# Two-layer hybrid decoder trunk on one core: modulation weights in a load ring of their own, weight tiles in a ring of five, stores put off

## The chip, the cores and the metric

The kernel runs on 1 core of one Trainium2 chip. The metric is the device time of one execution in microseconds (us); several runs are taken and their median is quoted. A profiled execution is a single one; its span is the time from its first to its last instruction.

## What is computed

Two layers over 256 tokens of width 2048, batch 1, all in float32. Each layer normalises its input, scales and shifts it by vectors that come from a conditioning vector `c` ("adaLN"), projects it, runs two mixers side by side on the result, merges them and adds the residual:

```python
def hybrid_layer(x, c_act, pos, norm_w, ada_w, ada_b, w_in, ret_gn_w, sinks, w_ret_o, w_swa_o, w_out):
    shift, scale, gate = jnp.split(c_act @ ada_w + ada_b, 3, axis=-1)
    u = rms_norm(x, norm_w) * (1.0 + scale[:, None, :]) + shift[:, None, :]
    proj = u @ w_in
    rq, rk, rv, rg, sq, sk, sv, sg, mg_ret, mg_swa = jnp.split(proj, offsets, axis=-1)
    ...
    ret_y = r @ w_ret_o          # r: chunkwise retention, group norm, SiLU gate
    ...
    swa_y = (a * jax.nn.silu(sg)) @ w_swa_o   # a: sliding-window attention with sinks
    merged = jax.nn.sigmoid(mg_ret) * ret_y + jax.nn.sigmoid(mg_swa) * swa_y
    return x + gate[:, None, :] * (merged @ w_out)
```

`c_act` is `silu(c)`, and the trunk ends with one more RMS norm. `ada_w` is 2048 x 6144 per layer, `w_in` 2048 x 15360, and the three output projections are 2048 x 2048 each.

## The kernel before, in words

**Weight steps.** The products with the weights are cut into chunks of 512 output columns, and a chunk into steps of two 128-row blocks of the weight (`steps`; in the sliced chunks some have one block). A step loads one tile of 128 x 1024 float32 (512 KB) from DRAM, and `prep` (L291) splits it into an upper half `w_hi` (ACT, L118) and a lower half `w_lo` = tile - upper half (DVE, L115). `gemm` (L307) then issues three products per pair of halves: 12 matmuls of 512 columns where tokens are the output's rows (token-major) and 24 of 256 where features are (feature-major: `qk`, `sq`, `sk`, `sg`). `prep` runs `LOOKAHEAD` = 3 steps ahead of the matmuls, and `w_hi` and `w_lo` have four buffers each.

**Order of chunks in a layer.** First the retention's twelve chunks (`qk`, `rg`, `rv` four times), in slices over the input features (four slices in layer 0, two in layer 1), so that the first products can start before all modulation vectors are there. Then `mr` (4 chunks), `ro` (4), `sk`, `sv`, `sq` and `sg` (4 each, in turn), `ms` (4), `so` (4), `wo` (4). The last chunk of `wo` is done half by half (`gemm_halves`, L343), so that the norm of the next layer can begin.

**Modulation.** `c_act @ ada_w` is done on the DVE: a unit is a 128 x 1024 tile of the transposed `ada_w`, multiplied by `c_act` and summed along its row (the reduce, L245). There are 192 units: 64 for layer 0's scale and shift, 32 for its gate, 64 for layer 1's scale and shift, 32 for its gate. `ada_block` (L214) issues a unit's load and its reduce together. `run_background` (L140), called after each step, issues them at a pace per step (`PACE`, `ada_pace`), beside the retention heads and the attention heads.

**Rings.** Pool tiles of one name share a ring of buffers, and a load waits until the buffer's last reader is done. Weight tiles and modulation tiles have the same name and pool,

```python
raw = state.get("ada_pool", wpool).tile([P, TK * NC], F32, name="w_raw")
SP.dma_start(out=raw, in_=src[i, :, h * 1024:(h + 1) * 1024])
```

with four buffers; only the 64 units of layer 0's scale and shift use a pool of eight (`adaraw`, which closes before the last slice).

**Queues.** Every DMA is issued by SP, in one list. The program's text is not the engines' order: the framework's scheduler lists each engine's instructions, and puts one that could run in an earlier gap of that engine, by its own estimates; on the chip each engine goes through its list strictly in order, waiting at each entry.

**Stores and fetches beside this.** `merge_first` (L648) stores the gated retention product `y1d[c]`; `merge_second` (L654) fetches it again in the output stage; the residual of layer 0 is stored in `hres` (L859) and fetched in layer 1.

Of the kernel before, what the change touches and what calls it, by code (L numbers as in the profile page):

```python
# [10 lines left out]
F32 = mybir.dt.float32  # L11
# [6 lines left out]
P = 128  # L18
# [14 lines left out]
PACE = (0.1, 0.6, 0.15, 0.4)  # L33

# [38 lines left out]
def trunk(ctx: ExitStack, tc: tile.TileContext, x, c2, earlyc, latec, win, wro, wso, wout, sinks, fnw, decayT,  # L73
# [8 lines left out]
    wpool, small = pool("wpool", 4), pool("small", 2)  # L82
    dpool = pool("dpool", space=DRAM)
# [46 lines left out]
    # ---------------------------------------------------------------- background work  # L130
# [60 lines left out]
    # ---------------------------------------------------------------- adaLN vectors  # L191
# [20 lines left out]
    gates = [dpool.tile([D], F32, name=f"gates{l}") for l in range(L)]  # L212

    def ada_block(key, l, src):  # L214
        nf = src.shape[0]
        part = small.tile([P, 32, 2], F32, name="ada_part")
        k0, k1 = (0, KT) if key[0] == "gate" else slice_bounds(l)[key[2]]

        def finish(f0, f1):
            p0, p1 = part[:, f0:f1, 0], part[:, f0:f1, 1]  # L220
            if key[0] == "gate":
                tt(p0, p0, p1, ALU.add)
                tt(p0, p0, adab_t[:, l, 32 + f0:32 + f1], ALU.add)
                ps = bank()
                PE.transpose(ps[0:KT, 0:P], p0, ident)
                row = small.tile([KT, P], F32, name="gate_row", bufs=1)
                ACT.activation(row, ps[0:KT, 0:P], AF.Copy)
                release(ps)
                SP.dma_start(out=gates[l].rearrange("(k p) -> k p", p=P), in_=row)
                return  # L230
            ks = slice(k0 + f0 // 2, k0 + f1 // 2)
            b = adab_t[:, l, 0:32].rearrange("p (a k) -> p k a", a=2)[:, ks, :]
            p0, p1 = (p.rearrange("p (k a) -> p k a", a=2) for p in (p0, p1))
            tt(p0, p0, b, ALU.add)
            tt(p0, p0, p1, ALU.add)
            DVE.scalar_tensor_tensor(out=scale[:, l, ks], in0=p0[:, :, 1], scalar=1.0, in1=norm_t[:, l, ks],
                                     op0=ALU.add, op1=ALU.mult)
            DVE.tensor_copy(out=shift[:, l, ks], in_=p0[:, :, 0])

        for f in range(0, nf, 2):  # L240
            for h in range(2):
                for i in (f, f + 1):
                    raw = state.get("ada_pool", wpool).tile([P, TK * NC], F32, name="w_raw")
                    SP.dma_start(out=raw, in_=src[i, :, h * 1024:(h + 1) * 1024])
                    DVE.tensor_tensor_reduce(out=raw, in0=raw, in1=c_row[:, h * 1024:(h + 1) * 1024], scale=1.0, scalar=0.0,  # L245
                                             op0=ALU.mult, op1=ALU.add, accum_out=part[:, i, h:h + 1])
                    yield 1.25
            if key == ("mod", 0, 0):
                finish(f, f + 2)
        if key != ("mod", 0, 0):  # L250
            finish(0, nf)
        done.add(key)
# [21 lines left out]
    # ---------------------------------------------------------------- products with the weights  # L274
# [15 lines left out]

    def prep(upto):  # L291
        while progress["prep"] < min(upto, len(steps)):
            i = progress["prep"]
            n, k, nk = steps[i]
            raw = wpool.tile([P, TK * NC], F32, name="w_raw")[:, 0:nk * NC]
# [11 lines left out]
    def gemm(act, ps=None):  # L307
# [6 lines left out]
        while progress["step"] < len(steps) and steps[progress["step"]][0] == n:  # L314
# [24 lines left out]
            run_background(STEP_BUDGET * nk / TK)  # L339
        flush()  # L340
        return ps

    def gemm_halves(act, finish):  # L343
# [3 lines left out]
        for t in range(2):  # L347
            ps = bank()
            for x in range(count):
# [3 lines left out]
                for j in range(TK):  # L353
                    kk = steps[i][1] + j
                    ah, al = (a[:, kk % 4, t * P:(t + 1) * P] for a in act[kk // 4])
                    for m, (a, w) in enumerate(((ah, hi), (al, hi), (ah, lo))):
                        mm(ps, a, w[:, j * NC:(j + 1) * NC],
                           x == 0 and j == 0 and m == 0, x == count - 1 and j == TK - 1 and m == 2)
                if t == 0:
# [7 lines left out]
    # ---------------------------------------------------------------- norm and modulation  # L367
# [32 lines left out]
    # ---------------------------------------------------------------- retention  # L400
# [101 lines left out]
    # ---------------------------------------------------------------- sliding-window attention  # L502
# [139 lines left out]
    # ---------------------------------------------------------------- gates and merges  # L642
# [5 lines left out]
    def merge_first(c, ps):  # L648
# [3 lines left out]
        SP.dma_start(out=y1d[c], in_=tokens(y))  # L652

    def merge_second(pl, c, ps, m_parts):  # L654
        yield from until(lambda: c == 0 or ("merged", c - 1) in keep)
        y1 = pl.tile([P, 1024], F32, name="stage", bufs=2)
        SP.dma_start(out=tokens(y1), in_=y1d[c])
        y = keep.pop(("ms", c))
        tt(y, ps, y, ALU.mult)
        tt(y, y, y1, ALU.add)  # L660
# [11 lines left out]
    # ---------------------------------------------------------------- schedule  # L672
# [4 lines left out]
    def ada_enqueue(key):  # L677
        ada_queue.append(ada_block(key, key[1], blocks[key]))
# [19 lines left out]
    with tc.tile_pool(name="start", bufs=1) as sp, tc.tile_pool(name="adaraw", bufs=8) as state["ada_pool"]:  # L698
        xt = [sp.tile([P, 2, NC], F32, name=f"x{c}") for c in range(4)]
        sums = sum_tiles()  # L700
        SP.dma_start(out=early, in_=earlyc)
        for _ in range(4):
            ada_turn()
        for c in range(4):
            SP.dma_start(out=xt[c], in_=xpart(c))
# [59 lines left out]
    for l in range(L):  # L765
# [65 lines left out]
        with tc.tile_pool(name=f"out{l}", bufs=1) as pl:  # L831
            m_parts = act_tiles(pl, "m")
            pace[0] = PACE[3]
# [11 lines left out]
            for c in range(4):  # L845
# [7 lines left out]
                def residual(t, ps, c=c, gr=gr, res=res):  # L853
# [4 lines left out]
                    if not last:  # L858
# [101 lines left out]
```

## Time and profile before

| what | value |
|---|---|
| runs | 2109.76, 2109.99, 2112.79 us; median 2109.99 us |
| span of the profiled execution | 2108.1 us |
| busy: PE, DVE, ACT, POOL | 2027.6, 1464.3, 1072.4, 19.1 us |
| moved by DMA | 480.78 MB, 228 GB/s in the mean |
| DMA issues of 512 KB weight tiles / modulation tiles | 660 / 192 |

The profiled execution's own time is the first to the last record; the runs are timed without a profile, and their median is 1.9 us longer than that span. PE is TensorE's matmul, DVE VectorE, ACT ScalarE, POOL GpSimd, SP SyncE. Matmuls are pipelined: a 512-column matmul is listed with some 0.39 us, and the next one starts 0.23 us after it.

### The profile page before, as it was taken

How to read it: one execution, taken by the hardware profiler on the slowest of the kernel's cores; microseconds unless marked ns; L12 is line 12 of the kernel's file. 1: busy time of each engine (PE TensorE's matmuls, PEld its weight loads, DVE VectorE, ACT ScalarE, POOL GpSimd, SP SyncE). 2: the span in 40 equal slices, each digit the busy share in tenths (PEclk: the TensorE clock that was granted, in tenths of full speed). 3: DMA queues.
4: the chain of work that ended last, by engine and by line, in shares of the span. 5: the costliest groups of instructions: out<-in, count | busy, mean ns of one | idle time of the engine just before them, and what ended most of it. 6: DMA issues, size and time to landing. Idle time of an engine off the chain costs nothing.

```text
span 2108.1 us, 30062 instructions
## 1 busy us (share of the span) xinstructions
PE 2027.6 (96%) x11482; PEld 1762.2 (84%) x11482; DVE 1464.3 (69%) x2115; ACT 1072.4 (51%) x1493; POOL 19.1 (1%) x28
## 2 busy tenths in 40 slices
PE   5999999999999999999998999999989999999998
PEld 3888888877899998877777898888778999988886
DVE  5899997666777777677656668864666677764555
ACT  4643556433465667534453545553334676674443
POOL 0000000000000000000000000000000000000000
PEclk7999999999999999999999999999999999999999
DMA  8989656678765666778868855556887554557664
GB/s 312 348 313 374 200 181 201 194 263 288 269 205 183 197 193 196 230 258 271 292 215 274 286 189 178 175 188 216 274 279 250 172 159 151 160 184 239 206 208 151
DMA packets 136595, 480.78 MB, mean 228 GB/s; under 512 B 15202, under 2 KB 15362, under 8 KB 136324
## 3 DMA queue, kind: packets, MB, share of 16 engines
q1 hardware_dynamic: 136452, 478.87, 68.5%
q8 instruction: 90, 1.47, 0.3%
q14 instruction: 53, 0.43, 0.1%
HBM read 470.41 MB, written 8.40 MB: 227 GB/s over the span
## 4 chain that ended last, share of the span: by engine, by line
PE 72%; DMA 15%; DVE 6%; issue 4%; ACT 2%; POOL 0%; SPq 0%; DVEq 0%; POOLq 0%; ACTq 0%
PE ps_mm L107 66%; DMA w_raw<-in_ada 10%; PE ps L107 4%; DVE w_lo L115 3%; DMA w_raw<-in_win 3%; ACT w_hi L118 2%; DMA w_raw<-in_wout 1%; DVE w_raw L245 1%; DMA w_raw<-in_wro 1%; PE ps L613 1%; PE ps L388 1%; DMA x<-in_x 0%; DVE sig L115 0%; ACT ps L370 0%; DVE sks L115 0%
## 5 line engine op out<-in xcount | busy, mean ns | idle before, releaser
L118 ACT ACTIVATE w_hi<-w_raw 128x1024 fp32r<-128x1024 f32 (+1 forms) x676 | 703.4, 1043 | 832.0 <-PE ps_mm L107 439.1
L115 DVE TENSOR_TENSOR w_lo<-w_raw,w_hi 128x1024 fp32r<-128x1024 f32 (+1 forms) x676 | 810.7, 1204 | 367.8 <-ACT w_hi L118 363.8
L107 PE MATMUL ps_mm<-uh,w_lo 128*128 128x256 f32 x1664 | 472.2, 284 | 8.5 <-DVE w_lo L115 8.3
L107 PE MATMUL ps_mm<-uh,w_hi 128*128 128x256 f32 x1664 | 472.7, 284 | 0.3 <-ACT w_hi L118 0.2
L107 PE MATMUL ps_mm<-ul,w_hi 128*128 128x256 f32 x1664 | 470.7, 283 | 0.0
L107 PE MATMUL ps_mm<-w_lo,uh 128*128 128x512 f32 x1088 | 429.7, 395 | 10.6 <-DVE w_lo L115 10.3
L107 PE MATMUL ps_mm<-w_hi,uh 128*128 128x512 f32 x1088 | 430.2, 395 | 2.4 <-ACT w_hi L118 2.4
L107 PE MATMUL ps_mm<-w_hi,ul 128*128 128x512 f32 x1088 | 427.4, 393 | 0.0
L245 DVE CUSTOM_DVE_ANT_0 w_raw<-w_raw,c_row 128x1024 f32<-128x1024 f32 x192 | 234.4, 1223 | 170.6 <-DMA w_raw<-in_ada 161.8
L107 PEld LDWEIGHTS ps_mm<-uh,w_lo 128*128 128x128 f32 x1664 | 319.0, 192 | 10.9 <-DVE w_lo L115 10.9
L107 PEld LDWEIGHTS ps_mm<-uh,w_hi 128*128 128x128 f32 x1664 | 319.0, 192 | 2.1 <-ACT w_hi L118 0.7
L107 PEld LDWEIGHTS ps_mm<-ul,w_hi 128*128 128x128 f32 x1664 | 319.0, 192 | 1.4
L107 PEld LDWEIGHTS ps_mm<-w_lo,uh 128*128 128x128 f32 x1088 | 206.0, 189 | 62.3 <-DVE w_lo L115 19.2
L107 PEld LDWEIGHTS ps_mm<-w_hi,uh 128*128 128x128 f32 x1088 | 206.5, 190 | 44.5 <-ACT w_hi L118 4.1
L107 PEld LDWEIGHTS ps_mm<-w_hi,ul 128*128 128x128 f32 x1088 | 206.5, 190 | 41.0
L107 PE MATMUL ps_mm<-w_lo,rah 128*128 128x512 f32 x512 | 202.8, 396 | 15.3 <-DVE w_lo L115 15.0
L107 PE MATMUL ps_mm<-w_hi,rah 128*128 128x512 f32 x512 | 201.9, 394 | 1.1 <-ACT w_hi L118 1.1
L107 PE MATMUL ps_mm<-w_hi,ral 128*128 128x512 f32 x512 | 200.3, 391 | 0.0
L107 PEld LDWEIGHTS ps_mm<-w_lo,rah 128*128 128x128 f32 x512 | 96.5, 188 | 43.9 <-DVE w_lo L115 23.7
L107 PEld LDWEIGHTS ps_mm<-w_hi,rah 128*128 128x128 f32 x512 | 96.7, 189 | 20.9 <-ACT w_hi L118 1.9
L107 PEld LDWEIGHTS ps_mm<-w_hi,ral 128*128 128x128 f32 x512 | 96.7, 189 | 20.1
L107 PE MATMUL ps_mm<-w_lo,mh 128*128 128x512 f32 x192 | 75.9, 395 | 0.0
(150 smaller groups left out, 1662.7 us busy)
## 6 DMA issues: line engine op xcount, KB each, us to landing
w_raw<-in_win SPq DMA_DIRECT2D x468, 512.0 KB, 4.2
w_raw<-in_ada SPq DMA_DIRECT2D x192, 512.0 KB, 5.5
w_raw<-in_wro SPq DMA_DIRECT2D x64, 512.0 KB, 4.9
w_raw<-in_wso SPq DMA_DIRECT2D x64, 512.0 KB, 3.6
w_raw<-in_wout SPq DMA_DIRECT2D x64, 512.0 KB, 4.7
w_raw<-in_win SPq DMA_DIRECT2D x24, 256.0 KB, 3.9
y1d<-sig SPq DMA_DIRECT2D x8, 512.0 KB, 5.4
stage<-y1d SPq DMA_DIRECT2D x8, 512.0 KB, 5.2
```

The costliest lines, as they stand in the source:

```text
L107: PE.matmul(o, lhsT=lhsT, rhs=rhs, start=start, stop=stop, skip_group_check=True)
L115: DVE.tensor_tensor(out=o, in0=a, in1=b, op=op)
L118: ACT.activation(hi, src, AF.Copy)
L245: DVE.tensor_tensor_reduce(out=raw, in0=raw, in1=c_row[:, h * 1024:(h + 1) * 1024], scale=1.0, scalar=0.0, op0=ALU.mult, op1=ALU.add, accu ...
L388: PE.transpose(ps[:, j * S + t * P:j * S + (t + 1) * P], h[:, t, (2 * i + j) * P:(2 * i + j + 1) * P], ident)
L613: PE.transpose(pt[:, h * P:(h + 1) * P], p[:, h, c0 * P:(c0 + 1) * P], ident)
```

## The change

Five things change.

- Modulation tiles get pools of their own: `ada_raw` in `adapool` (three buffers), still eight in the start's pool. `ada_load` issues the next load of a list `loads`; `ada_ahead`, called after each reduce, keeps up to two loads (seven in the start) ahead of the reduces.
- Weight tiles `w_raw` get a pool `rawpool` of five buffers; `w_hi` and `w_lo` keep four each.
- Stores of `y1d`, and of `hres` but for the last chunk, are issued two steps later (`defer`, `store_due`).
- The fetches of `y1d` for chunks 0 and 1 are issued at the head of the output stage, those for 2 and 3 after the merges of 0 and 1 (`fetch_first`).
- In the start, four modulation loads are issued first, then the four x loads, then the reduces. The area for descriptors that POOL would write shrinks (`dynamic_dma_scratch_size=1024`).

```diff
+RAW_BUFS, ADA_BUFS = 5, 3
+STORE_DELAY = 2
...
     wpool, small = pool("wpool", 4), pool("small", 2)
+    rawpool, adapool = pool("rawpool", RAW_BUFS), pool("adapool", ADA_BUFS)
...
+    def ada_load():
+        key, src, i, h = loads.popleft()
+        early_pool = state.get("ada_pool") if key[:2] == ("mod", 0) else None
+        raw = (early_pool or adapool).tile([P, TK * NC], F32, name="ada_raw")
+        SP.dma_start(out=raw, in_=src[i, :, h * 1024:(h + 1) * 1024])
+        loaded.append((key, i, h, raw))
+
+    def ada_ahead():
+        while loads:
+            key = loads[0][0]
+            if key[:2] == ("mod", 0):
+                held = sum(1 for k, *_ in loaded if k[:2] == ("mod", 0))
+                if held >= state["early_bufs"] - 1:
+                    return
+            elif sum(1 for k, *_ in loaded if k[:2] != ("mod", 0)) >= ADA_BUFS - 1:
+                return
+            ada_load()
...
-                    raw = state.get("ada_pool", wpool).tile([P, TK * NC], F32, name="w_raw")
-                    SP.dma_start(out=raw, in_=src[i, :, h * 1024:(h + 1) * 1024])
+                    if not loaded:
+                        ada_load()
+                    *unit, raw = loaded.popleft()
                     DVE.tensor_tensor_reduce(out=raw, in0=raw, in1=c_row[:, h * 1024:(h + 1) * 1024], scale=1.0, scalar=0.0,
                                              op0=ALU.mult, op1=ALU.add, accum_out=part[:, i, h:h + 1])
+                    ada_ahead()
                     yield 1.25
...
+    def defer(out, in_):
+        deferred.append([STORE_DELAY, out, in_])
+
+    def store_due(all_of_them=False):
+        for d in deferred:
+            d[0] -= 1
+        while deferred and (all_of_them or deferred[0][0] <= 0):
+            _, out, in_ = deferred.popleft()
+            SP.dma_start(out=out, in_=in_)
...
-            raw = wpool.tile([P, TK * NC], F32, name="w_raw")[:, 0:nk * NC]
+            raw = rawpool.tile([P, TK * NC], F32, name="w_raw")[:, 0:nk * NC]
...
             run_background(STEP_BUDGET * nk / TK)
+            store_due()
...
-        SP.dma_start(out=y1d[c], in_=tokens(y))
+        defer(y1d[c], tokens(y))
+
+    def fetch_first(pl, c):
+        y1 = pl.tile([P, 1024], F32, name="stage", bufs=2)
+        SP.dma_start(out=tokens(y1), in_=y1d[c])
+        keep["y1", c] = y1
...
-        y1 = pl.tile([P, 1024], F32, name="stage", bufs=2)
-        SP.dma_start(out=tokens(y1), in_=y1d[c])
         y = keep.pop(("ms", c))
         tt(y, ps, y, ALU.mult)
-        tt(y, y, y1, ALU.add)
+        tt(y, y, keep.pop(("y1", c)), ALU.add)
+        if c < 2:
+            fetch_first(pl, c + 2)
...
+        state["early_bufs"] = 8
...
         for _ in range(4):
+            ada_load()
+        for c in range(4):
+            SP.dma_start(out=xt[c], in_=xpart(c))
+        for _ in range(4):
             ada_turn()
         for c in range(4):
-            SP.dma_start(out=xt[c], in_=xpart(c))
...
-                    if not last:
+                    if not last and c < 3:
+                        defer(hres[c][:, t, :], o)
+                    elif not last:
                         SP.dma_start(out=hres[c][:, t, :], in_=o)
...
-    nc = bacc.Bacc("TRN2", target_bir_lowering=False, num_devices=1)
+    nc = bacc.Bacc("TRN2", target_bir_lowering=False, num_devices=1, dynamic_dma_scratch_size=1024)
```

**What moves on the DVE at the start.** The DVE's list from the 13th reduce of a modulation unit to the first lower halves. A reduce is an `ISA` row that reads `w_raw` (after the change `ada_raw`) and `c_row`, with a second row that stores its sum in `ada_part`. Before:

```order
L245 ISA w_raw_221,ada_part_220<-w_raw_221,c_row_92 128x1024
L245 ISA ada_part_220 128x1
L115 TENSOR_TENSOR ul0_237<-u32_252,uh0_236 128x256
L115 TENSOR_TENSOR w_lo_227<-w_raw_224,w_hi_226 128x1024
L727 TENSOR_SCALAR nsink_t_234<-sink_t_232 128x64
L115 TENSOR_TENSOR w_lo_266<-w_raw_263,w_hi_265 128x512
L115 TENSOR_TENSOR w_lo_272<-w_raw_269,w_hi_271 128x1024
```

After the change:

```order
L273 ISA ada_raw_212,ada_part_240<-ada_raw_212,c_row_98 128x1024
L273 ISA ada_part_240 128x1
L118 TENSOR_TENSOR ul0_257<-u32_272,uh0_256 128x256
L273 ISA ada_raw_215,ada_part_240<-ada_raw_215,c_row_98 128x1024
L273 ISA ada_part_240 128x1
L273 ISA ada_raw_218,ada_part_240<-ada_raw_218,c_row_98 128x1024
...
L273 ISA ada_raw_234,ada_part_240<-ada_raw_234,c_row_98 128x1024
L273 ISA ada_part_240 128x1
L273 ISA ada_raw_242,ada_part_240<-ada_raw_242,c_row_98 128x1024
L273 ISA ada_part_240 128x1
L118 TENSOR_TENSOR w_lo_247<-w_raw_244,w_hi_246 128x1024
L780 TENSOR_SCALAR nsink_t_254<-sink_t_252 128x64
```

One reduce stood here ahead of the first `w_lo`; now eight do (three of them in the rows left out). SP's list has 13 modulation loads ahead of the first weight load before, and 20 after.

**What moves on SP in layer 0's `ro`.** SP's list in the first chunks of `ro`; `in_wro` is a weight tile, `in_ada4` the gate's units of layer 0, `in_ada5` layer 1's first scale and shift. Before:

```order
L296 DMA w_raw_4085<-in_wro 128x1024
L296 DMA w_raw_4106<-in_wro 128x1024
L244 DMA w_raw_4124<-in_ada4 128x1024
L296 DMA w_raw_4127<-in_wro 128x1024
L244 DMA w_raw_4145<-in_ada4 128x1024
L296 DMA w_raw_4148<-in_wro 128x1024
L652 DMA y1d0_113<-sig_3252 128x1024
L296 DMA w_raw_4166<-in_wro 128x1024
L244 DMA w_raw_4184<-in_ada4 128x1024
L296 DMA w_raw_4187<-in_wro 128x1024
L296 DMA w_raw_4205<-in_wro 128x1024
L244 DMA w_raw_4223<-in_ada4 128x1024
```

After the change:

```order
L226 DMA ada_raw_6815<-in_ada5 128x1024
L337 DMA w_raw_4074<-in_wro 128x1024
L337 DMA w_raw_4095<-in_wro 128x1024
L226 DMA ada_raw_7121<-in_ada5 128x1024
L337 DMA w_raw_4115<-in_wro 128x1024
L226 DMA ada_raw_7366<-in_ada5 128x1024
L337 DMA w_raw_4136<-in_wro 128x1024
L337 DMA w_raw_4158<-in_wro 128x1024
L226 DMA ada_raw_7586<-in_ada5 128x1024
L337 DMA w_raw_4176<-in_wro 128x1024
L226 DMA ada_raw_7813<-in_ada5 128x1024
L337 DMA w_raw_4197<-in_wro 128x1024
```

The share of modulation loads is about the same, but they belong to a later block, and the two kinds no longer take each other's slots. Counted on the lists, a weight load's slot used to come free two `w_lo` ahead of that tile's own, and now four.

**What moves on the DVE in layer 0's `sq` and `sg`.** The DVE's list over the same attention work (`src`, `sp` and `ses` belong to the heads' softmax). Before:

```order
L115 TENSOR_TENSOR w_lo_6458<-w_raw_6455,w_hi_6457 128x1024
L245 ISA w_raw_6557,ada_part_5071<-w_raw_6557,c_row_92 128x1024
L245 ISA ada_part_5071 128x1
L115 TENSOR_TENSOR w_lo_6494<-w_raw_6491,w_hi_6493 128x1024
L115 TENSOR_TENSOR src0_6728<-ssm0_6486,ses0_6449 128x8
L598 RECIPROCAL src0_6728<-src0_6728 128x8
L115 TENSOR_TENSOR sp0_6235<-sp0_6235,src0_6728 128x4x256
L115 TENSOR_TENSOR w_lo_6530<-w_raw_6527,w_hi_6529 128x1024
L115 TENSOR_TENSOR src1_6766<-ssm1_6522,ses1_6453 128x8
L598 RECIPROCAL src1_6766<-src1_6766 128x8
L115 TENSOR_TENSOR sp1_6282<-sp1_6282,src1_6766 128x4x256
```

After the change:

```order
L118 TENSOR_TENSOR w_lo_6468<-w_raw_6465,w_hi_6467 128x1024
L273 ISA ada_raw_13275,ada_part_10767<-ada_raw_13275,c_row_98 128x1024
L273 ISA ada_part_10767 128x1
L273 ISA ada_raw_13335,ada_part_10767<-ada_raw_13335,c_row_98 128x1024
L273 ISA ada_part_10767 128x1
L118 TENSOR_TENSOR w_lo_6504<-w_raw_6501,w_hi_6503 128x1024
L118 TENSOR_TENSOR src0_6738<-ssm0_6496,ses0_6459 128x8
L273 ISA ada_raw_13374,ada_part_10767<-ada_raw_13374,c_row_98 128x1024
L273 ISA ada_part_10767 128x1
L118 TENSOR_TENSOR w_lo_6540<-w_raw_6537,w_hi_6539 128x1024
L641 RECIPROCAL src0_6738<-src0_6738 128x8
L273 ISA ada_raw_13395,ada_part_10767<-ada_raw_13395,c_row_98 128x1024
```

One reduce stood in this piece before; four stand there now, between the same lower halves.

## Rows read from the trace of the kernel before

**Rows 1.** The page: busy time by engine, and PE's share in 40 slices.

```profile
PE 2027.6 (96%) x11482; PEld 1762.2 (84%) x11482; DVE 1464.3 (69%) x2115; ACT 1072.4 (51%) x1493; POOL 19.1 (1%) x28
...
PE   5999999999999999999998999999989999999998
```

**Rows 2.** Waits of all engines: engine, line, waited for, us in total, times, longest.

```profile
PE ps_mm L107 <- DVE w_lo L115: 33.7, 36, 3.1
...
DVE w_raw L245 <- DMA w_raw<-in_ada: 161.8, 98, 4.8
...
SPq L296 <- DVE w_lo L115: 1075.3, 527, 6.8
...
SPq L244 <- DVE w_lo L115: 141.0, 92, 6.6
```

**Rows 3.** The page: DMA issues, KB each, median us from issue to landing.

```profile
w_raw<-in_ada SPq DMA_DIRECT2D x192, 512.0 KB, 5.5
```

**Rows 4.** Chain of waits: start us, us, work; undisturbed runs of steps.

```profile
609.06 25.92 PE ps_mm L107 x216
...
1886.11 59.88 PE ps_mm L107 x264
```

**Rows 5.** Stretches: length, busy time by engine, granted PE clock, DMA share, GB/s.

```profile
core 0: us, PE busy (x) PEld busy (x) DVE busy (x) ACT busy (x) POOL busy (x), PEclk, DMA share, GB/s
20.00:30.00 10.00, 3.59 (x12) 2.12 (x12) 7.96 (x20) 6.55 (x12) 1.11 (x1) 0.50 1.03 404
160.00:200.00 40.00, 40.00 (x223) 35.08 (x222) 38.45 (x48) 14.88 (x14) 0.00 (x0) 1.00 1.00 383
414.58:565.63 151.05, 138.08 (x673) 113.45 (x672) 97.80 (x113) 55.34 (x56) 0.00 (x0) 0.99 0.80 269
1458.64:1613.16 154.52, 140.18 (x674) 114.15 (x672) 97.82 (x113) 55.35 (x56) 0.00 (x0) 0.98 0.79 267
871.12:1037.66 166.54, 161.42 (x706) 131.03 (x705) 109.27 (x125) 66.12 (x73) 0.00 (x0) 0.98 0.82 274
1918.62:2076.37 157.75, 157.75 (x706) 129.52 (x704) 92.30 (x87) 69.95 (x76) 0.00 (x0) 1.00 0.67 216
1037.66:1063.10 25.44, 24.14 (x97) 17.47 (x96) 17.93 (x23) 13.06 (x18) 0.56 (x1) 1.00 0.81 276
2076.37:2098.68 22.31, 22.31 (x97) 17.90 (x95) 10.12 (x16) 4.92 (x9) 0.55 (x1) 1.00 0.16 55
1072.83:1220.20 147.37, 140.19 (x782) 119.86 (x782) 93.23 (x111) 70.23 (x81) 0.00 (x0) 0.99 0.77 257
565.63:769.56 203.93, 203.93 (x1682) 202.39 (x1681) 149.96 (x278) 131.66 (x241) 0.00 (x0) 1.00 0.61 199
```

**Rows 6.** Timeline of DVE at the edge between the layers.

```profile
1063.10 1.23 DVE L245 CUSTOM_DVE_ANT_0 w_raw<-w_raw,c_row 128x1024 f32<-128x1024 f32 x1 [1.73 <-DMA w_raw<-in_ada]
...
1066.53 1.22 DVE L245 CUSTOM_DVE_ANT_0 w_raw<-w_raw,c_row 128x1024 f32<-128x1024 f32 x1 [0.87 <-DMA w_raw<-in_ada]
```

**Rows 7.** Timeline of DVE, then of PE, at the start.

```profile
29.94 1.22 DVE L245 CUSTOM_DVE_ANT_0 w_raw<-w_raw,c_row 128x1024 f32<-128x1024 f32 x1
...
31.08 1.22 DVE L245 CUSTOM_DVE_ANT_0 w_raw<-w_raw,c_row 128x1024 f32<-128x1024 f32 x1
...
32.68 1.22 DVE L245 CUSTOM_DVE_ANT_0 w_raw<-w_raw,c_row 128x1024 f32<-128x1024 f32 x1
...
33.91 0.42 DVE L115 TENSOR_TENSOR ul<-u,uh 128x256 fp32r<-128x256 f32 x1
34.85 1.23 DVE L115 TENSOR_TENSOR w_lo<-w_raw,w_hi 128x1024 fp32r<-128x1024 f32 x1 [0.52 <-ACT w_hi L118]
...
36.13 0.79 PE L107 MATMUL ps_mm<-w_lo,uh 128*128 128x512 f32 x1
```

More of the change, by code (lines that the diff above doesn't have):

```diff
@@ L212, in trunk, with ada_order @@
     gates = [dpool.tile([D], F32, name=f"gates{l}") for l in range(L)]
+    loads, loaded = deque(), deque()
+    def ada_order(nf):
+        return [(i, h) for f in range(0, nf, 2) for h in range(2) for i in (f, f + 1)]
+    def ada_load():
[14 more added lines that the diff above has]
+            ada_load()
     def ada_block(key, l, src):
@@ L242, in ada_block @@
                 for i in (f, f + 1):
-                    raw = state.get("ada_pool", wpool).tile([P, TK * NC], F32, name="w_raw")
-                    SP.dma_start(out=raw, in_=src[i, :, h * 1024:(h + 1) * 1024])
+                    if not loaded:
+                        ada_load()
+                    *unit, raw = loaded.popleft()
+                    assert unit == [key, i, h]
                     DVE.tensor_tensor_reduce(out=raw, in0=raw, in1=c_row[:, h * 1024:(h + 1) * 1024], scale=1.0, scalar=0.0,
                                              op0=ALU.mult, op1=ALU.add, accum_out=part[:, i, h:h + 1])
+                    ada_ahead()
                     yield 1.25
@@ L289, in trunk @@
     ready = {}
+    deferred = deque()
+    def defer(out, in_):
[6 more added lines that the diff above has]
+            SP.dma_start(out=out, in_=in_)
     def prep(upto):
@@ L358, in gemm_halves @@
                            x == 0 and j == 0 and m == 0, x == count - 1 and j == TK - 1 and m == 2)
+                store_due()
                 if t == 0:
@@ L677, in ada_enqueue @@
     def ada_enqueue(key):
+        loads.extend((key, blocks[key], i, h) for i, h in ada_order(blocks[key].shape[0]))
         ada_queue.append(ada_block(key, key[1], blocks[key]))
@@ L832, in trunk @@
             m_parts = act_tiles(pl, "m")
+            for c in range(2):
+                fetch_first(pl, c)
             pace[0] = PACE[3]
```

## Prediction

> **What bounds the kernel now.** I read the page's shares first: PE is busy for 2027.6 of 2108.1 us, and the slices show where it is not, in slice 1 and in three stretches of 8s and 9s [rows 1]. Then the waits: PE's longest is for a lower half, `w_lo`; behind it the DVE stood 161.8 us before 98 reduces because an `in_ada` tile had not landed, and SP stood mostly until the DVE had freed a `w_raw` slot [rows 2]. So the stall is a ring: weight tiles and modulation tiles share four slots, and where 0.6 modulation units go with each step, a slot comes back after 4 / 1.6 = 2.5 steps, though a load takes 5.5 us to land [rows 3] and a step 2.72 (token-major, 59.88 / 22) to 2.88 us (feature-major, 25.92 / 9) [rows 4]. The reader is to see it in twins: the same `so` and `wo` steps take 166.54 us in layer 0 beside reduces, and 157.75 us in layer 1 without, where PE is busy for all of it [rows 5].
>
> **The sum, on the profiled execution (span 2108.1 us; the median of the runs is 1.9 us longer).**
>
> *What the order shows beyond the diff.* The matmuls keep their order. On the DVE, however, the reduces no longer queue for weight slots, and all 192 come in layer 0. Counted against the weight tiles (684 in all), tiles 76 to 143 (last slice, `mr`) now hold 36 reduces instead of 3; 144 to 191 (`ro`, `sk`, `sv`) 31 instead of 28; 192 to 255 (`sq`, `sg`) 55 instead of 10; layer 1 none instead of 59.
>
> *Layer 1, `ro` to `sv`.* 40 steps of 2.72 and 8 of 2.88 are 131.8 us; it took 154.52 [rows 4, 5], so 22.7 lost. All 28 reduces leave. I keep 1.5 us of it, as even a stage without stalls has some transposes and evacuations: gain 21, bounds 15 and 22.7.
>
> *Layer 1, first slice.* 32 x 2.72 + 16 x 2.88 = 133.1 us, taken 147.37 [rows 4, 5]: 14.3 lost. 28 reduces leave; about 2 us are transposes and a half-speed clock after the layer's edge, which stay: gain 12, bounds 8 and 14.3.
>
> *Layer 0, `so` and `wo`.* 8.8 us against its twin, and 25.44 - 22.31 = 3.1 in the half-by-half product [rows 5]. Three reduces are left there: gain 11.5, bounds 8 and 11.9. The stores put off by two steps, and the fetch of `y1d` made at the stage's start, are inside this term: in the twin they stand in the old places and PE loses nothing, so apart from the reduces I cost them at zero. Should reduces return there, the DVE's wait for a fetched tile would show again.
>
> *Edge between the layers.* Two reduces with their waits (1.73 + 1.15 and 0.87 + 1.15 us) stand ahead of the last residual and of the reciprocal root [rows 6]. The residual could have started some 0.9, the root some 1.2 us sooner: gain 2, bounds 0 and 4.9.
>
> *Layer 0, `ro` to `sv`.* Lost 151.05 - 131.8 = 19.2 us [rows 4, 5]. Here the reduces stay; only the ring changes. A weight load is now freed four `w_lo` ahead of its use, 4 x 2.72 = 10.9 us against 5.5 to land. A modulation load is freed two ahead, 5.4 us, so the DVE may still stand some half a microsecond per reduce; but it is busy for 97.80 of 151.05 us [rows 5], and a weight no longer waits behind it. Gain 15, bounds 5 and 19.2.
>
> *The start, a loss.* Before, 13 loads and reduces of modulation units come ahead of the first weight tile; now 20 do, since seven are kept ahead and the DVE's list places them when they are first able to run. The 13th reduce starts at 32.68 and the first `w_lo` at 34.85 us, and PE's first use of it is at 36.13 [rows 7]. Seven more reduces, 1.15 us apart as in [rows 7], stand between: 8.0 us, less 0.5 us for which that `w_lo` had waited for its upper half. The 20th load needs the slot of the 12th unit, free at 32.3, lands before 38 and is wanted at 41: no wait. Nothing covers this, because PE has no other work, and the later slices run at PE's rate: loss 7.4, bounds 4 (if the later slices give part back) and 9.
>
> *The dense DVE, a loss.* In `sq`/`sg` the DVE is busy for 149.96 of 203.93 us beside 10 or 11 reduces [rows 5]; 45 more at 1.15 us are 51.8, together 201.7. Busy time counts neighbours that overlap by some 0.08 us, 278 of them, so the true spare is between 2 and 24 us. An in-order engine this full passes some waits to PE. Before, PE lost nothing at 38.45 of 40.00 us of DVE [rows 5], so I am nearer to that row than to a full queue: loss 6 for this and the 33 added reduces of the slice before, bounds 0 and 30.
>
> *Edits at nothing.* The smaller descriptor area pays for four more tiles; POOL moves nothing (19.1 us, 28 instructions [rows 1]). The first x loads keep their place in SP's list. The two-step delay keeps a `sig` slot longer, but the next writer comes a whole chunk later.
>
> Sum: 21 + 12 + 11.5 + 2 + 15 - 7.4 - 6 = 48.1 us off. 2108.1 - 48.1 = 2060.0, and with the 1.9 outside the span **2062 us** in the median.
>
> *A rule against the change.* A DMA limit would take part of it back. The densest stretch now has 14 reduces to 12 weight tiles, 26 x 0.524 = 13.6 MB in 33.4 us of PE time; DMA moved 404 GB/s while the queue was deep and 383 with PE full [rows 5], by which it takes 33.7 to 35.6 us, within what eight slots hold. The Trainium skill (DMA: Bandwidth & Descriptors, Where 436 GB/s comes from) says that the HBM side, about 358 GB/s, binds loads into SBUF. By that figure the stretch would take 38.1 us, an estimate of some 5 us more; the trace disagrees with its 404 and 383, and the sum leaves it out.
>
> **The rivals.**
>
> *A. The DVE becomes the bound of `sq`/`sg`.* Mechanism as above with the upper price: about 20 us more, 2082. For it: 201.7 of 203.93 by busy time. Against it: the 95% stretch that cost PE nothing.
>
> *B. Slower: reduces that wait for their loads inside a full DVE.* If each of the 55 reduces in `sq`/`sg` waits as the 98 did on average (161.8 / 98 = 1.65 us [rows 2]), that is 91 us less some 2 of spare, and the result is 2062 - 6 + 89 = 2145, 35 slower. It decides from about (48 + 6 + 2) / 55 = 1.0 us of wait per reduce on. Against it: these loads now have slots of their own and are issued two reduces ahead.
>
> *C. No gain in layer 0, since transfers and not slots are the limit.* If 267 to 274 GB/s, what the stalled stages moved [rows 5], is all there is, tiles 144 to 255 with 86 reduces (198 x 0.524 = 103.8 MB) need 387 us instead of about 336: 2062 + 51 = 2113, just slower. Against it: 383 and 404 elsewhere.
>
> *D. Loads bound by the 358 GB/s limit in the one dense stretch, worked from its 13.6 MB:* 2067.
>
> **How the numbers follow.** Forecast 0.69, A 0.19, B 0.05, C 0.03, D 0.04. All gains at their upper bounds with a start loss of 4 would be 2110 - 73 + 4 = 2041, less likely; all lower ones with the start at 9 and the dense stretch at 30 would be 2110 - 36 + 39 = 2113. A range of **2046 to 2086** leaves out B, C and the ends of the forecast and of A, in all about 2 in 10. About 0.2%, 4 us, is what a measurement of this kernel can tell from no change. Forecast, A and D are faster; B slower; C is split between the last two: faster 0.92, same 0.02, slower 0.06.
>
> **What would show it.** Right: the first `w_lo` near 42 us and PE's first use of it near 43.5; no `in_ada` load in layer 1; the twins of `ro` to `sv` near 133 to 136 us; PE waits for `w_lo` down from 33.7 to under 8; DVE near 95% in `sq`/`sg` with PE still full. Wrong: PE waiting in `sq`/`sg` for DVE results by more than 10 us (A, B), DVE waits for `in_ada` above 1 us each there (B), or layer 0's `ro` still near 150 us with DMA at its share of 0.8 (C).

## The result and the profile after

The changed kernel took 2075.9 us in the median of four runs (2072.95 to 2080.3), the kernel before 2110.34 beside it: a ratio of 0.9833, 95% interval 0.9818 to 0.9849. The forecast was 2062, with a range of 2046 to 2086. The profiled execution is the fastest of the four, 2072.95 us with a span of 2071.0.

The page of the changed kernel, where [rows 1] answer:

```profile
PE 2010.0 (97%) x11482; PEld 1761.7 (85%) x11482; DVE 1457.5 (70%) x2115; ACT 1068.6 (52%) x1493; POOL 21.6 (1%) x28
...
PE   3999999999999999999999999999999999999998
```

The 8s are gone from PE's slices except for the last one, and the first slice fell from 5 to 3. The stretches between the same instructions as in [rows 5], with the same columns: layer 0's slices up to the last slice's final two chunks; these two chunks and `mr`, called "last slice and `mr`" from here on; `ro` to `sv`; `sq`/`sg`; `so` and `wo` 0 to 2; the half-by-half product and the edge; then layer 1's slices with `mr`, and its `ro` to `sv`:

```profile
40.21:305.54 265.33, 262.84 (x1533) 232.39 (x1534) 233.51 (x323) 129.68 (x159) 3.06 (x2) 0.99 0.87 306
305.54:429.36 123.82, 119.19 (x561) 98.68 (x559) 116.11 (x197) 61.33 (x83) 6.77 (x6) 0.97 0.81 276
429.36:566.94 137.58, 134.24 (x673) 112.57 (x672) 99.22 (x122) 56.20 (x58) 0.00 (x0) 1.00 0.88 308
566.94:781.28 214.34, 207.18 (x1682) 203.98 (x1681) 197.04 (x369) 128.72 (x237) 0.00 (x0) 0.99 0.87 299
882.85:1040.86 158.01, 158.01 (x706) 129.35 (x705) 90.72 (x83) 70.37 (x77) 0.00 (x0) 1.00 0.72 232
1040.86:1070.81 29.95, 26.76 (x118) 21.32 (x116) 14.57 (x23) 12.81 (x23) 1.11 (x2) 0.94 0.58 195
1070.81:1444.16 373.35, 373.35 (x2085) 327.40 (x2086) 230.98 (x293) 192.15 (x225) 5.53 (x8) 1.00 0.59 181
1444.16:1576.02 131.86, 131.86 (x674) 113.15 (x673) 68.67 (x60) 56.44 (x58) 0.00 (x0) 1.00 0.66 208
```

Two of these stretches of the kernel before are not in [rows 5]; they are the last slice with `mr`, and layer 1's slices with `mr`:

```profile
300.01:414.58 114.57, 114.57 (x561) 96.52 (x559) 84.74 (x135) 61.67 (x80) 5.86 (x6) 1.00 0.61 197
1072.83:1458.64 385.81, 378.63 (x2085) 327.78 (x2085) 264.61 (x355) 191.98 (x225) 5.53 (x8) 1.00 0.65 214
```

Against the terms of the prediction (us; each is the difference of the lengths of two such stretches):

| term | forecast | measured |
|---|---|---|
| layer 1, `ro` to `sv` | +21 | 154.52 - 131.86 = +22.7 |
| layer 1, first slice | +12 | 385.81 - 373.35 = +12.5 (both slices and `mr`) |
| layer 0, `so`, `wo`, and the edge | +11.5 + 2 | 8.5 + 5.2 = +13.7 |
| layer 0, `ro` to `sv` | +15 | 151.05 - 137.58 = +13.5 |
| start (to the end of the first stretch) | -7.4 | 300.01 - 305.54 = -5.5 |
| dense DVE: last slice and `mr`, `sq`/`sg` | -6 | -9.3 - 10.4 = **-19.7** |
| sum | 48.1 | 37.1 (span 2108.1 - 2071.0; the rows add up to 37.2) |

All gains came. The dense stretches ate 13.7 us more than forecast. In these two stretches the DVE's timeline has 27 reduces (3 before) and 56 (10 before); the prediction's 36 and 55 are counted by tiles, and its last slice is the whole one. The waits, where [rows 2] answer:

```profile
DVE ada_raw L273 <- DMA ada_raw<-in_ada: 60.2, 42, 5.3
...
PE ps_mm L110 <- DVE w_lo L118: 5.1, 6, 1.4
...
PE ps L110 <- DVE pl L118: 3.7, 4, 1.6
...
PE ps L110 <- DVE sqs L581: 3.5, 2, 3.2
...
PE ps L110 <- ACT sh L121: 3.1, 2, 2.7
```

PE hardly waits for a lower half any more (33.7 before). New, or nearly so, are waits for the heads' own small products (`sh`, `sqs`, `pl`), and the DVE still stood 60.2 us before reduces whose tile had not landed. How one becomes the other is to be seen at 397 us, in the timeline of the DVE, then of PE:

```profile
393.15 1.22 DVE L118 TENSOR_TENSOR w_lo<-w_raw,w_hi 128x1024 fp32r<-128x1024 f32 x1
397.00 1.22 DVE L273 CUSTOM_DVE_ANT_0 ada_raw<-ada_raw,c_row 128x1024 f32<-128x1024 f32 x1 [2.63 <-DMA ada_raw<-in_ada]
...
399.29 0.55 DVE L118 TENSOR_TENSOR s<-ps,dec 128x384 f32<-128x384 f32 x1
...
397.32 0.39 PE L110 MATMUL ps_mm<-w_lo,uh 128*128 128x512 f32 x1
400.45 0.38 PE L110 MATMUL ps<-rvh,sh 128*128 128x256 f32 x1 [2.74 <-ACT sh L121]
```

A reduce at the head of the DVE's list waits 2.63 us for its tile. Behind it stand a lower half and `s`, from which ACT makes `sh`, which PE multiplies: PE stands 2.74 us. Then the clock (windows, the last three columns are granted clock, DMA share, GB/s):

```profile
400.00:405.00 5.00, 3.80 (x15) 3.30 (x16) 4.68 (x8) 2.78 (x4) 0.00 (x0) 0.60 0.83 275
405.00:410.00 5.00, 5.00 (x20) 4.16 (x19) 4.44 (x18) 0.55 (x1) 2.29 (x2) 0.71 1.00 384
410.00:415.00 5.00, 5.00 (x25) 4.09 (x24) 4.30 (x9) 3.40 (x7) 0.00 (x0) 1.00 0.78 278
401.10:407.80 6.70, 6.10 (x22) 5.32 (x23) 6.31 (x16) 2.38 (x3) 0.84 (x1) 0.50 0.94 340
602.50:605.80 3.30, 3.30 (x18) 3.30 (x17) 3.24 (x5) 1.72 (x3) 0.00 (x0) 0.50 0.96 344
```

After that pause PE was granted 0.60 and 0.71 of full speed in the mean, a mixture of the 1.2 and the 2.4 GHz level. In the 6.7 us from 401.10 on it had the 1.2 GHz level alone and was busy for 6.10 us, which is 0.50 x 6.10 = 3.1 us more, as much again as the pause. The last row is the same after a pause in `sq`/`sg`: 0.50 x 3.30 = 1.7 us more. So of the 19.7 us, PE was idle for 4.6 and 7.2 (length less PE's busy time), and for 7.9 it was busy longer at the same work; the lower clock makes 3.1 + 1.7 = 4.8 of these.

In `sq`/`sg` PE paused five times, 7.1 us in all. Two of these pauses (4.3 us) stood behind a reduce that had just waited more than 2 us for its tile; the first of them, in the timeline of the DVE, then of PE:

```profile
599.02 1.23 DVE L273 CUSTOM_DVE_ANT_0 ada_raw<-ada_raw,c_row 128x1024 f32<-128x1024 f32 x1 [2.13 <-DMA ada_raw<-in_ada]
...
602.17 0.81 PE L110 MATMUL ps<-sks,sqs 128*128 128x256 f32 x3 [3.17 <-DVE sqs L581]
```

The other three (2.8 us) stood behind reduces close together, with no wait of more than 0.3 us among them.

### The profile page after: what moved, and what is told of

Its sections match the earlier page's. It is cut to its first block, busy times and chain, and to the rows that moved or that the text cites. A ratio compares the mean times of both kernels' runs of the same rounds, so it can differ in the third digit from the quotient of the medians.

```text
span 2071.0 us, 29986 instructions
## 1 busy us (share of the span) xinstructions
PE 2010.0 (97%) x11482; PEld 1761.7 (85%) x11482; DVE 1457.5 (70%) x2115; ACT 1068.6 (52%) x1493; POOL 21.6 (1%) x28
## 4 chain that ended last, share of the span: by engine, by line
PE 83%; DVE 7%; DMA 5%; issue 3%; ACT 1%; POOL 0%; SPq 0%; DVEq 0%; POOLq 0%; ACTq 0%
PE ps_mm L110 77%; DMA ada_raw<-in_ada 5%; PE ps L110 4%; DVE w_lo L118 3%; DVE ada_raw L273 2%; PE ps L656 1%; PE ps L431 1%; DMA x<-in_x 0%; DVE rot L118 0%; ACT ps L413 0%; DVE sig L118 0%; SPq L337 0%; DVE sks L118 0%; DVE pl L118 0%; POOL rs_r L424 0%
## 5 line engine op out<-in xcount | busy, mean ns | idle before, releaser
L273 DVE CUSTOM_DVE_ANT_0 ada_raw<-ada_raw,c_row 128x1024 f32<-128x1024 f32 x192 | 232.7, 1220 | 69.4 <-DMA ada_raw<-in_ada 60.2
```

## The experiments

Median times are compared; the kernel before ran beside each set, at 2110 to 2115 us. From here on "held" means that a reduce is listed behind the lower half (`w_lo`) that precedes it in the program's text, an order in the DVE's list and no wait.

**1. Late reduces held to the program's pace.** Rings, start and stores stay as changed.

```diff
-            split(hi, lo, raw)
+            lower.append(split(hi, lo, raw).ins)
...
+                    with (tc.issue_after(lower[-1]) if key[:2] != ("mod", 0) else nullcontext()):
                         DVE.tensor_tensor_reduce(out=raw, in0=raw, ...)
```

> The changed kernel (2075.9 us), with every modulation reduce from layer 0's gate on held behind the lower half that precedes it in the program's text, so that the reduces stand where they stood before (31 in tiles 76 to 143 become 3, 54 in tiles 192 to 255 become 10, layer 1 gets 63 back); rings, start and stores stay. Theory (dense DVE: reduces bunched in layer 0, some waiting for their loads, cost about 9 us in the last slice and mr and 10 us in sq and sg): these two stretches fall back from 123.8 to about 115 and from 214.3 to about 204 us, while layer 1, which gets reduces again, loses some 5 us in ro to sv and 5 in its first slice, and layer 0's so and wo 2: about 2069 us. Rival (the new rings or the transfers cost it, not the place of the reduces): the two stretches stay near 124 and 214, and the time goes up by what layer 1 loses, to about 2085.

2051.67 us (2049.11 to 2054.1), ratio to before 0.9713 (0.9698 to 0.9729): 24 us less than the changed kernel. The last slice with `mr`, `ro` to `sv`, `sq`/`sg`; layer 1's slices, its `ro` to `sv`:

```profile
306.42:420.99 114.57, 114.57 (x561) 96.52 (x559) 84.94 (x135) 61.70 (x80) 5.87 (x6) 1.00 0.63 196
420.99:552.85 131.86, 131.86 (x674) 113.13 (x672) 100.54 (x118) 56.47 (x58) 0.00 (x0) 1.00 0.91 313
552.85:756.77 203.92, 203.92 (x1682) 202.38 (x1681) 147.45 (x272) 130.78 (x240) 0.00 (x0) 1.00 0.63 197
1046.31:1422.78 376.47, 375.11 (x2086) 327.84 (x2085) 265.78 (x359) 192.12 (x225) 5.55 (x8) 1.00 0.69 221
1422.78:1554.64 131.86, 131.86 (x674) 113.15 (x672) 100.55 (x118) 56.47 (x58) 0.00 (x0) 1.00 0.89 309
```

Both dense stretches are back at their old lengths, and `ro` to `sv` has PE busy throughout in both layers, though 28 reduces stand in each. The theory was right on the dense stretches and too dark on layer 1: it expected 10 us of loss there, and 3.1 came. The 5.7 us that `ro` to `sv` gave back in layer 0 it had not named. With the new rings, reduces at the program's pace cost PE almost nothing: in the timeline of the DVE, from the first weight tile on, one reduce waits for its tile, 0.2 us, and PE is idle for 1.4 us in layer 1's slices.

**2. Is it the number of reduces, or their waits for tiles?** Two kernels hold each late reduce at the very place where the changed kernel's list has it. One leaves out the loads, so those reduces read `c_row` twice; the other keeps the loads and reduces 32 of 1024 columns.

```diff
-    DVE.tensor_tensor_reduce(out=raw, in0=raw, in1=c_row[...], ...)
+    row = c_row[:, h * 1024:(h + 1) * 1024]
+    DVE.tensor_tensor_reduce(out=raw, in0=raw if key[:2] == ("mod", 0) else row, in1=row, ...)
```

> The changed kernel, with each reduce from layer 0's gate on held at the very place where the changed kernel's list has it, but reading c_row twice in place of a modulation tile, so that its load (128 of 192) and every wait for one leaves; the scale, shift and gate so made are not the reference's. Theory W (what costs is that a reduce stands in the in-order list until its tile has landed): the last slice and mr fall from 123.8 to about 115, ro to sv from 137.6 to 132, sq and sg from 214.3 to about 204 us, and the time is about 2051. Theory D (the number of reduces alone costs it, since 33 and 45 more of them fill the DVE): the first and the last of these stretches stay above 120 and 210, and the time is above 2065.

2051.7 us (2051.65 to 2051.87), ratio 0.9712 (0.9693 to 0.9732). Last slice with `mr`, `ro` to `sv`, `sq`/`sg`:

```profile
307.18:424.71 117.53, 115.89 (x560) 96.48 (x559) 114.59 (x196) 60.81 (x81) 6.78 (x6) 1.00 0.58 180
424.71:556.57 131.86, 131.86 (x673) 113.15 (x672) 103.50 (x127) 56.47 (x58) 0.00 (x0) 1.00 0.66 207
556.57:760.31 203.74, 203.74 (x1683) 202.37 (x1682) 193.37 (x364) 129.31 (x237) 0.00 (x0) 1.00 0.54 166
```

The last row decides: the DVE is busy for 193.37 of 203.74 us, and PE for all of it. A DVE that is 95% full costs PE nothing in `sq`/`sg`, and in the last slice with `mr` 3.0 of the 9.3 us, where nothing in its list waits for a modulation tile. The traffic of those loads leaves with the waits, though (166 GB/s instead of 299); the next run keeps it.

> The changed kernel, with each reduce from layer 0's gate on held at the very place where the changed kernel's list has it and with every load, but working on 32 of the tile's 1024 columns (some 0.1 instead of 1.15 us); the scale, shift and gate so made are not the reference's. Theory D (density): the last slice and mr fall to about 115 and sq and sg to about 204 us, and the time is about 2055. Theory W (waits for loads inside the list): the DVE still waits for modulation tiles by 50 us or more in all, and as a shorter reduce only makes it arrive at them sooner, the stretches stay above 119 and 209, and the time is above 2063.

2056.26 us (2051.25 to 2057.92), ratio 0.973 (0.9707 to 0.9752); waits, and `sq`/`sg`:

```profile
DVE ada_raw L280 <- DMA ada_raw<-in_ada: 101.8, 62, 5.4
```

```profile
553.49:763.09 209.60, 205.97 (x1683) 203.93 (x1682) 145.28 (x369) 130.35 (x240) 0.00 (x0) 0.99 0.88 304
```

The waits rose from 60.2 to 101.8 us, as theory W said, but an emptier DVE absorbed most of them, with 304 GB/s moved: the last slice with `mr` came back to 114.57, `ro` to `sv` to 131.86, and `sq`/`sg` kept 5.7 of its 10.4 us. The time is D's number, the waits are W's; its bound of 2063 was missed. The two runs together say that neither the waits nor the density alone makes the whole loss: of the 19.7 us the full list without waits keeps 3.0, the waits in an emptier list 5.7. What fits both is that a wait inside the list costs what the list has no room to catch up.

**3. Why does a reduce with a slot of its own wait?** In the changed kernel's `ro`, the timeline of SP, then of the DVE:

```profile
433.77 0.42 SPq L226 DMA_DIRECT2D ada_raw<-in_ada  x1
434.52 5.40 SPq L337 DMA_DIRECT2D w_raw<-in_wro  x2
439.98 0.42 SPq L226 DMA_DIRECT2D ada_raw<-in_ada  x1
...
437.20 1.23 DVE L273 CUSTOM_DVE_ANT_0 ada_raw<-ada_raw,c_row 128x1024 f32<-128x1024 f32 x1 [2.70 <-DMA ada_raw<-in_ada]
...
438.35 1.22 DVE L118 TENSOR_TENSOR w_lo<-w_raw,w_hi 128x1024 fp32r<-128x1024 f32 x1
440.57 1.23 DVE L273 CUSTOM_DVE_ANT_0 ada_raw<-ada_raw,c_row 128x1024 f32<-128x1024 f32 x1 [1.00 <-DMA ada_raw<-in_ada]
```

The load at 439.98 stands in SP's list behind two weight loads, of which the second is out only at 439.92. A weight load waits for the slot that a `w_lo` frees, and the `w_lo` at 438.35 stood behind a reduce that had waited 2.70 us for its own load. The two lists, SP's and the DVE's, hold each other up. To test it, ACT issues the late modulation loads; the reduces are held no earlier than in the changed kernel's list.

```diff
-        SP.dma_start(out=raw, in_=src[i, :, h * 1024:(h + 1) * 1024])
+        (SP if key[:2] == ("mod", 0) else ACT).dma_start(out=raw, in_=src[i, :, h * 1024:(h + 1) * 1024])
```

> The changed kernel, with each reduce from layer 0's gate on held no earlier than where the changed kernel's list has it, and with these modulation loads issued by ACT instead of SP, so that none stands behind a weight load that waits for its slot; in ro to sv the reduces stand within one weight tile of the changed kernel's places (in sq and sg some drift later). In the changed kernel the DVE stood 37.9 us before 22 of the reduces in ro to sv. Theory S (SP's list: the modulation load goes out late because a weight load ahead of it waits for a slot, which a lower half frees, which stands behind the reduce): these waits fall below 10 us, ro to sv from 137.6 to at most 134, and the time to about 2060. Rival (the transfer itself takes longer than the list allows for): the waits stay above 25 us, ro to sv at 136 or more, and the time above 2070.

2070.37 us (2065.12 to 2072.21), ratio 0.9786 (0.9767 to 0.9805). `ro` to `sv`, and `sq`/`sg`:

```profile
432.38:564.24 131.86, 131.86 (x673) 113.13 (x672) 105.93 (x131) 56.34 (x57) 0.00 (x0) 1.00 0.93 335
564.24:779.24 215.00, 208.73 (x1682) 206.42 (x1681) 181.47 (x338) 127.14 (x228) 0.00 (x0) 0.98 0.78 259
```

In `ro` to `sv`, summed over the timeline of the DVE, the waits fell from 37.9 us (22 reduces) to 3.0 (2), and the stretch lost nothing: SP's list was the cause there. The Trainium skill (DMA: Bandwidth & Descriptors, Issuing engines are not separate DMA queues) says that issuing from several engines saves only the issue time. Here it saved 5.7 us in one stretch, and by the waits that left it is the order of the list that gained. In the last slice with `mr` (123.85 us) and in `sq`/`sg` it gained nothing; in the latter six waits of 14.8 us stayed. ACT's list holds loads there among its own work; which part of that loss is ACT's was not tried, and the expected 2060 was missed by 10.

**4. The start.** Three kernels: the early reduces held as in 1; only one load ahead until the first weight tile; and, on top of experiment 1, no load ahead of its reduce for all of layer 0's scale and shift (64 units), as in the kernel before.

```diff
-        state["early_bufs"] = 8
+        state["early_bufs"] = 1
```

> The changed kernel with only the modulation reduces of layer 0's scale and shift held behind the lower half that precedes them in the program's text: 13 stand ahead of the first lower half instead of 20, but SP's list still has 20 modulation loads ahead of the first weight load. Theory of the prediction (the seven reduces in the DVE's list make the start late): the first lower half comes near 35 us instead of 41.54, and the time falls by 5 to 6, to about 2070. Rival (SP's list makes it late: the first weight load stands behind the 20th modulation load, which waits for a slot, and is issued at 31.99 instead of 21.12 us): the first lower half comes near 40.2, and the time falls by only 1, to about 2074.5.

> The changed kernel, keeping one modulation load ahead instead of seven until the first weight tile has been prepared: 14 loads and 14 reduces stand ahead of it, before 13 and 13, in the changed kernel 20 and 20. Both theories of the start expect the first weight load near 22 us, the first lower half near 36 and about 5 us less than the changed kernel: 2071. If neither list is the reason and the deeper ring is (eight slots full of transfers ahead of the weight), the first lower half stays near 41 and the time near 2076.

> The kernel with late reduces held to the program's pace (2051.7 us), and also no modulation load ahead of its reduce while layer 0's scale and shift are made, so that 13 loads and 13 reduces stand ahead of the first weight tile, as before. Theory (the start's loss is SP's list and goes with it): PE's first matmul on a weight near 35 us and 6 us less, about 2045. Rival (the loss only moves, as where the load ahead was put off until the first weight tile: there PE started at 34.85 and stood later): the slices end near 306 us as now, and the time is about 2051.

Held: 2095.22 us, ratio 0.9927 (0.9911 to 0.9944), 19 slower than the changed kernel. Short: 2077.51, ratio 0.9838 (0.9822 to 0.9853), no change. None ahead: 2045.44 (2042.06 to 2046.07), ratio 0.968 (0.9659 to 0.97), 6 below experiment 1.

The changed kernel's timeline of SP, ACT and the DVE:

```profile
31.99 0.42 SPq L337 DMA_DIRECT2D w_raw<-in_win  x1
39.10 1.06 ACT L121 ACTIVATE w_hi<-w_raw 128x1024 fp32r<-128x1024 f32 x1 [5.96 <-DMA w_raw<-in_win]
41.54 1.22 DVE L118 TENSOR_TENSOR w_lo<-w_raw,w_hi 128x1024 fp32r<-128x1024 f32 x1
```

The first weight load went out at 31.99 (21.12 before), because SP's list has 20 modulation loads ahead of it and the 20th waits for a slot. With the seven reduces out of the way, the held kernel has its first lower half at 40.73, not near 35, and in front of it:

```profile
40.73 1.23 DVE L122 TENSOR_TENSOR w_lo<-w_raw,w_hi 128x1024 fp32r<-128x1024 f32 x1 [6.45 <-ACT w_hi L121]
```

So the rival of that run was right on the start. Its time of 2074.5 was not: later weight loads now stand behind modulation loads whose slots held reduces free late, and ACT's waits for `w_raw<-in_win` went from 20.3 to 76.5 us. In the short kernel PE began at 34.85, but seven reduces in a row came ahead of the sixth weight tile's lower half, and the last slice began at 306.40 as before. Without loads ahead PE began at 34.41 and the last slice at 299.76. At the start, where loads already had eight slots of their own, loading ahead only put more work in front of the weights.

**5. What in the rings does it?** On experiment 1, four weight slots; then, with the start of experiment 4: one ring of eight for both kinds, six and two slots, and seven and one. In the diff the slots are `RAW_BUFS, ADA_BUFS`:

```diff
-RAW_BUFS, ADA_BUFS = 5, 3
+RAW_BUFS, ADA_BUFS = 4, 3
```

> The kernel with late reduces held to the program's pace (2051.7 us), with four weight slots instead of five. Theory (what was needed is that modulation tiles no longer take weight slots: a weight slot then comes free three lower halves ahead, 3 x 2.72 = 8.2 us against 5.5 to land): about 2052, ro to sv near 132 us in both layers. Rival (the fifth slot is what covers the load): stalls come back in ro to sv, so and wo, 3 to 8 us in each, and the time is 2060 to 2080.

2059.4 us (2056.44 to 2061.54), ratio 0.9748 (0.9727 to 0.9769): 8 more than with five. Neither theory has it whole. `ro` to `sv` and `so` lose nothing, as the first said; layer 1's slices take 381.67 instead of 376.47 us.

> The paced kernel with the start as before (2045.4 us), with weight and late modulation tiles in one ring of eight slots in place of rings of five and three. Theory (slots were short, whoever owns them: 8 slots at 1.6 tiles per step are 5 steps or 13.6 us, against 5.5 to land): 2045, ro to sv near 132 us. Rival (a ring of their own is needed, because slots come back in the order in which they were taken and a modulation tile holds its slot until a later reduce): weight loads wait again, ro to sv and so lose 3 to 10 us each, and the time is 2055 to 2080.

2044.75 us (2043.06 to 2045.92), ratio 0.9668 (0.9652 to 0.9684); `ro` to `sv` 131.85 us, and the DVE waits for no modulation tile. With eight slots, they need no owner.

> The paced kernel with the start as before (2045.4 us), with six weight slots and two modulation slots. Theory (five slots cover nearly all, only the first slice of layer 1 still lost some 1 us): 2044, and with the reduces at the program's pace one load ahead is enough. Rival (with one load ahead the DVE waits for modulation tiles again): 20 us or more of such waits and a time of 2050 to 2060.

2043.71 us (2043.02 to 2045.84), ratio 0.9664 (0.9648 to 0.968): the same as 2045.44 within the runs. By the DVE's timeline 19 reduces wait 20 us in all, nearly all in layer 1's slices.

> The paced kernel with the start as before (2045.4 us), with seven weight slots and one modulation slot, so that no modulation load is ahead of its reduce. Theory (loading ahead is what takes the wait out of the DVE's list): in ro to sv a reduce comes every 4.5 us and a load takes 5.5 to 6 from the reduce before it, so the DVE waits 1 to 2 us before each, 80 us or more in all; seven weight slots hide part of it, and the time is 2050 to 2065. Rival (with weights in a ring of their own such waits cost nothing): 2045.

2115.13 us (2112.67 to 2118.47), ratio 1.0 (0.9989 to 1.0011): the whole gain is gone. The waits, and layer 0's `sq`/`sg` and layer 1's slices with `mr`:

```profile
DVE ada_raw L274 <- DMA ada_raw<-in_ada: 199.3, 91, 3.9
...
PE ps_mm L110 <- ACT uh L121: 26.4, 1, 26.4
PE ps_mm L110 <- DVE w_lo L122: 16.8, 18, 2.8
PE ps L251 <- DVE ada_part L118: 13.5, 2, 7.7
```

```profile
554.80:769.99 215.19, 207.59 (x1683) 205.65 (x1682) 156.30 (x288) 130.29 (x240) 0.00 (x0) 0.98 0.63 201
1059.75:1464.29 404.54, 376.94 (x2085) 329.15 (x2085) 265.32 (x359) 192.95 (x225) 5.54 (x8) 0.97 0.65 206
```

PE's waits for lower halves are only 16.8 us. The larger part is that the modulation itself comes too late: PE stands 26.4 us in layer 1's slices for `uh`, which needs the second half of layer 1's scale and shift, and 13.5 us in front of the transposes of the two gates. While PE stands there, the last reduces of that half come 5 us apart, each 3.3 to 3.8 us behind its load (DVE's timeline, 1209.70 to 1219.74): with one slot a load and a reduce take turns. From no load ahead (seven weight slots) to one (six) is worth 71 us, of which the spans are 68.8 apart and these waits make 39.9; from one to two ahead, with a weight slot less, these runs show no gain.

**6. The stores and the fetch alone,** on the kernel before, with its rings and its start.

> The kernel before with only the two-step delay of the stores, the early fetches of y1d and the smaller descriptor area; rings, loads and the start stay as before. The prediction's zero: 2110, within 4 us of the kernel before, with PE's waits for lower halves near 34 us. Rival (a store of y1d or hres that waits at the head of SP's list held up weight loads in layer 0's ro and so, and moving it is part of the gain): 3 to 8 us less, 2102 to 2107, with layer 0's ro to sv shorter than 151 us.

2112.58 us (2110.14 to 2119.58), ratio 1.0004 (0.9992 to 1.0016). Layer 0's `ro` to `sv` 148.76 us (2.3 less), `so` and `wo` 0 to 2 170.00 (3.5 more). The prediction's zero stands; the rival expected 3 to 8 less.

## Why the prediction was right, and where it was not

*What bounds the kernel* was right: slots and a load that was late. The four gains were forecast at 61.5 and measured at 62.3 us. Experiment 5 qualifies the reason: with eight slots and loads ahead of their reduces, two kinds may share a ring, and with rings of seven and one and no load ahead the time of the kernel before is back, though in part by a modulation that comes too late for PE. Four shared slots with loads ahead were not run, so how much of the old stall was the number of slots stays open.

*Layer 0, `ro` to `sv`*: forecast +15 on the ground that the DVE has room and may stand "some half a microsecond per reduce". It stood 37.9 us before 22 of the 30 reduces there, 1.3 us per reduce, but the DVE was busy for only 99.22 of 137.58 us and could catch up: 5.7 us of the stretch were lost. Experiment 1 shows that all 19.2 us could be had beside 28 reduces. (In layer 1 the 1.5 us that the prediction kept back came off too: 131.86 us are the steps alone.)

*The start*: the size was nearly right (7.4 forecast, 5.5 measured), the step was not. It counted seven reduces in the DVE's list, and said that the 20th load needs a slot that is free at 32.3 and so meets "no wait". But the first weight load stood behind that load in SP's list. The DVE's list gave the same time by chance: the first `w_lo` came at 41.54, and with the reduces gone still at 40.73. PE's first use of it was at 42.81, 6.7 us later than before; the slices gave 1.2 of them back.

*The dense DVE* is the step that failed: 6 us, and 19.7 came. It sits inside the bounds of 0 to 30 and is the size of rival A, but A's reason, that the DVE's busy time fills the stage, fell for `sq`/`sg` with the run without loads (95% busy, PE full); in the last slice with `mr` it may hold for 3.0 us. The mechanism of the rest is rival B's, waits for loads inside a full list. I had set it aside because "these loads now have slots of their own and are issued two reduces ahead". They are two ahead in the program's text. In SP's list they stand behind weight loads, and the DVE's list has each reduce as early as its load was estimated to land. In `sq`/`sg` 12 of 56 reduces waited 15.7 us, 0.28 us per reduce, against the 1.0 from which B would have made the kernel slower; PE's 7.2 us there stayed under the 10 that the prediction had named as a sign of A or B. Four tenths of the price, 7.9 us in which PE was busy for longer, 4.8 of them by the lower clock after its pauses, was in no term.

*Rival D's limit* of 358 GB/s (the Trainium skill, DMA: Bandwidth & Descriptors, Where 436 GB/s comes from) does not bind here: 384 GB/s in the window at 405 us above. *Rival C* is out by the same rows.

## What to carry to other kernels

A prefetch ring changes two things: when a load can start, and, where a scheduler lists instructions as soon as they seem ready, where its consumer stands. Give the load its lead and hold the consumer at the pace of the work it rides on; here that was worth 24 us on top of 34. Price a wait in an in-order list by the room behind it (37.9 us of waits cost 5.7 where the DVE was 72% busy; 19.7 us of waits stood in the stretches that lost 19.7 where it was over 90%, and all but 3.0 of that loss left with the loads), and read the issuing engine's list as well as the waiting engine's.

## What the runs showed that I had not expected

- A pause of 2.7 us of PE was followed by 6.7 us at the 1.2 GHz level, which cost 3.1 us more.
- Without the late modulation loads four runs lay within 0.22 us of each other (2051.65 to 2051.87); the changed kernel's lay within 7.4.
- The fastest versions with every load in place are the held ones with the old start: 2043.71 (six and two slots), 2044.75 (one ring of eight) and 2045.44 us (five and three), which these runs do not tell apart.
